# Bias and maximum ahead of copies and z on VectorE, and the last two attention units' turns and values each in one interruption

## The chip, the cores and the metric

The kernel runs on one core of one Trainium2 chip. The metric is the device time of one execution in microseconds (us). Of several runs the median is given. Engines are named as in the profile: PE is TensorE's matmuls, PEld its weight loads, DVE is VectorE, ACT is ScalarE, POOL is GpSimd, SP is the engine that issues most DMAs.

## The reference, cut to what matters

One step of an encoder layer over 320 positions (256 of a prompt, 64 of a running stream), model width 2048, all in float32:

```python
z = rmsnorm(x, ln_g) @ w_in                # 2048 -> 1024 q, 128 k, 128 v, 2 x 1024 gating (u, v)
# group A: 16 heads of 64, 2 key heads; chunks of 64 queries see their own chunk and the 2 before
s = q @ k * HEAD_DIM**-0.5 + bias          # bias: T5 relative positions
m = maximum(max(s), sink)
p = exp(s - m)
w = p / (sum(p) + exp(sink - m))
attn = w @ v
# group B: gelu(zs) -> u, v;  v = rmsnorm(v);  sgu = u * (W_s v + b), chunks of 128 positions
x = x + concat(rmsnorm(attn), rmsnorm(sgu)) @ w_out
x = x + square(relu(rmsnorm(x) @ w_up)) @ w_down
```

Outputs are x for both sets of positions, the new k and v rows, and the normalised v rows of the stream.

## The kernel before, in words

**Weight products.** Activations lie transposed, channels on the 128 partitions and the 320 positions along the free axis. Each matrix is split into a high and a low part. `products` works in pieces: a piece loads 512 rows by 256 columns of a weight (`w_raw`), ScalarE makes the high part (`w_hi`, line 116), VectorE the low part (`w_lo`, line 117), and TensorE runs 24 matmuls of 128x128 by 320 (line 144). There are three buffers each of `w_hi` and `w_lo`. A product of `w_in` has four pieces (96 matmuls) and accumulates in one of two pairs of PSUM banks (`acc`). The products run in the order: q (four, the first with k and v), v of the gating (g = 0 to 3, lines 562 to 571), u of the gating (g = 0 to 3, lines 646 to 665), then w_out, w_up and w_down.

**Interruptions.** `between_pieces` gives functions that run behind a piece: their narrow matmuls stand in TensorE's order between two pieces of weight matmuls. Both `tc.issue_after` and the list `narrow` fix an order of issue on one engine; they add no semaphore wait by themselves. Where nothing fixes it, a planner with a timeline model orders each engine's instructions.

**Attention.** It is done in 8 units: units 0 to 3 for the first key head, 4 to 7 for the second. Units 0 and 4 hold two chunks of queries (two `parts`), the others one. `attend(i)` does three steps of three units in one interruption: the turn of unit i−2 (12 transposes of its probabilities, line 503, into two PSUM banks from the pool `misc`, which has two), the scores of unit i (line 438, into the two score banks), and the values of unit i−3 (line 515, into columns 384 to 511 of the turn's banks, and of the score banks for a second part). Then VectorE adds the bias to the scores (line 460), takes the maximum (line 465) and forms the sink's exponent (`es`, line 466); ScalarE does the exponentials (line 471), POOL multiplies by the reciprocal of the sum (line 481); ScalarE copies values to `ao` (line 523) and VectorE copies the turned probabilities out of the banks to `pts` (line 527), which has two buffers.

`attend(0)` and `attend(1)` stand in the last q product, behind its second and fourth piece; `attend(2 g + 2)` and `attend(2 g + 3)` behind the second and fourth piece of the gating's v product g. So `attend(8)` (turn of unit 6, values of unit 5) stands behind the second piece of v product 3, `attend(9)` (turn of 7, values of 6) behind its fourth, and `attend(10)` (values of 7) behind the second piece of u product 1, together with `prompt_rows`.

**Gating.** `gelu2` reads a product's PSUM pair into z on VectorE (line 549) and alternates between ScalarE (551, 553) and VectorE (552, 554). Squares of v are summed on POOL (`add_square`, line 544), POOL scales v by its gain (line 571). `prompt_rows` turns the v of the two prompt blocks to rows in half-size transposes (`by_halves`, line 582): eight channel groups of block 0 into the misc banks, six of block 1 into the score banks. `by_rows`, one piece later, turns the remaining two of block 1 and the stream's by full transposes (line 599) and copies them out (line 601). `spatial` (lines 611 to 620) applies W_s a piece after that.

Of the kernel before, what the change touches and what calls it, by code (L numbers as in the profile page):

```python
# [11 lines left out]
AF = mybir.ActivationFunctionType  # L12
# [3 lines left out]
P = 128  # L16
# [15 lines left out]
def hymba_step_kernel(ctx: ExitStack, tc: tile.TileContext, i, o):  # L32
# [13 lines left out]
    def misc():  # L46
        return ps_m.tile([P, 512], F32, name="misc", tag="misc")

    def score_bank(p, name="s_ps"):
        return ps_sc.tile([P, 512], F32, name=f"{name}{p}", tag=f"s{p}")  # L50
# [367 lines left out]
    def parts(u):  # L418
        n0 = 0
        for w, (b, kv) in enumerate(groups[u]):  # L420
            yield (w, n0, kv) + blocks[b]
            n0 += len(blocks[b][4])

    probs, ready = {}, []
    room = blk("vnat", [P, 2560])
    vnat = room[:, 0:2048].rearrange("p (t c) -> p t c", t=2)

# [16 lines left out]
    def softmax(u, s_ps):  # L444
        ws = range(len(groups[u]))
        sinks_u = sinks_pj[:, None, :, 2 * groups[u][0][1]:2 * groups[u][0][1] + 2].to_broadcast([P, len(ws), 2, 2])
        if len(ws) == 2:
            nc.vector.tensor_copy(out=s_rows[:, :, :, 64:194:129].rearrange("x p j w -> x w p j"), in_=sinks_u)
        pr = at.tile([P, 2, 3, 2, HD], F32, name="pr", tag="pr", bufs=2)
        nm = at.tile([P, 2, 2, 2], F32, name="nm", tag="nm")  # L450
        den = at.tile([P, 2, 2, 2], F32, name="den", tag="den")
        es = at.tile([P, 2, 2, 2], F32, name="es", tag="es")
        at_col = lambda w: 193 - parts_of_u[w][5]  if w == len(ws) - 1 else 0
        parts_of_u = list(parts(u))
        for w, n0, kv, q0, k0, nk, b0, _ in parts_of_u:
            c = at_col(w)
            for p in range(2):
                for j in range(2):
                    h, at_ = 2 * kv + j, n0 * P + j * nk
                    nc.vector.scalar_tensor_tensor(out=s_rows[:, p, j, c:c + nk], in0=s_ps[p][:, at_:at_ + nk],  # L460
                                                   scalar=rq[:, r_at(h, q0 // HD, p):r_at(h, q0 // HD, p) + 1],
                                                   in1=bias[:, p, h, b0:b0 + nk], op0=ALU.mult, op1=ALU.add)
        for w, n0, kv, q0, k0, nk, b0, _ in parts_of_u:
            c = at_col(w)
            nc.vector.tensor_reduce(out=nm[:, w], in_=s_rows[:, :, :, c:c + nk + 1], axis=AX.X, op=ALU.max, negate=True)  # L465
        nc.vector.tensor_tensor(out=es[:, 0:len(ws)], in0=nm[:, 0:len(ws)], in1=sinks_u, op=ALU.add)
        for w, n0, kv, q0, k0, nk, b0, tiles in parts_of_u:
            c = at_col(w)
            for p in range(2):
                for j in range(2):  # L470
                    nc.scalar.activation(out=pr[:, p, n0:n0 + len(tiles), j],  # L471
                                         in_=s_rows[:, p, j, c:c + nk].rearrange("x (n k) -> x n k", k=HD), func=AF.Exp,
                                         bias=nm[:, w, p, j:j + 1], accum_out=den[:, w, p, j:j + 1])
        nc.scalar.activation(out=es[:, 0:len(ws)], in_=es[:, 0:len(ws)], func=AF.Exp)
        nc.vector.tensor_tensor(out=den[:, 0:len(ws)], in0=den[:, 0:len(ws)], in1=es[:, 0:len(ws)],
                                op=ALU.add)
        nc.vector.reciprocal(out=den[:, 0:len(ws)], in_=den[:, 0:len(ws)])
        for w, n0, kv, q0, k0, nk, b0, tiles in parts_of_u:
            ns = slice(n0, n0 + len(tiles))
            for p in range(2):  # L480
                ready[:] = [nc.gpsimd.tensor_tensor(out=pr[:, p, ns], in0=pr[:, p, ns],
                                                    in1=den[:, w, p, None, :, None].to_broadcast([P, len(tiles), 2, HD]),
                                                    op=ALU.mult).ins]
        probs[u] = pr

    def attend(i, beside=None):

        t, v = i - 2, i - 3
        n = len(groups)
        t, v = t if 0 <= t < n else None, v if 0 <= v < n else None  # L490
        bank = [misc(), misc()] if t is not None else [score_bank(r) for r in range(2)]
        s_ps = [score_bank(p) for p in range(2)] if i < n else None
        hs = [slice(r * HD, (r + 1) * HD) for r in range(2)]

        def behind(mms):
            with tc.issue_after(narrow[-1]):
                narrow.append([mm() for mm in mms][-1].ins)

        if t is not None:
            s = probs.pop(t)  # L500

            def turn(p, n, x):
                return nc.tensor.transpose(out=bank[x][:, (p * 3 + n) * HD:(p * 3 + n + 1) * HD],  # L503
                                           in_=s[hs[x], p, n].rearrange("x j k -> x (j k)"), identity=ident[hs[x], hs[x]])

            behind([lambda p=p, n=n, x=x: turn(p, n, x) for p in range(2) for n in range(3) for x in range(2)])
        if s_ps:
            behind([lambda: scores(i, s_ps)])
        if beside:
            with tc.issue_after(narrow[-1]):  # L510
                outs = beside(bank)
        if v is not None:
            side = {w: [b[:, 384:512] for b in (s_ps if w else bank)] for w in range(len(groups[v]))}
            behind([lambda w=w, n0=n0, n=n, x=x, kv=kv, ts=ts, j=j, p=p:
                    nc.tensor.matmul(out=side[w][j][hs[p]], lhsT=vz[hs[j], x, kv], rhs=pts[v % 2][hs[j], :, p, n0 + n],  # L515
                                     start=n == 0, stop=n == len(ts) - 1)
                    for w, n0, kv, _, _, _, _, ts in parts(v) for n, x in enumerate(ts) for j in range(2) for p in range(2)])
        if s_ps:
            softmax(i, s_ps)
        if v is not None:  # L520
            for w, _, kv, q0, *_ in parts(v):
                for j in range(2):
                    nc.scalar.activation(out=ao[:, 4 * kv + 2 * j:4 * kv + 2 * j + 2, q0:q0 + 64],
                                         in_=side[w][j].rearrange("p (a q) -> p a q", a=2), func=AF.Copy)
        if t is not None:
            for x in range(2):
                nc.vector.tensor_copy(out=pts[t % 2][:, x],
                                      in_=bank[x][:, 0:384].rearrange("k (p n q) -> k p n q", p=2, n=3))

        if beside:  # L530
            for out in outs:
                out()
# [11 lines left out]
            nc.gpsimd.tensor_tensor(out=acc[:, 0:T], in0=acc[:, 0:T], in1=sq, op=ALU.add)  # L544


    def gelu2(ps, out):
        z = sm.tile([P, 2, T], F32, name="z", tag="w2", bufs=4)
        nc.vector.tensor_tensor(out=z, in0=ps[:, :, 0:T], in1=rx[:, None, :].to_broadcast([P, 2, T]), op=ALU.mult)
        c = sm.tile([P, 2, T], F32, name="gc", tag="w2", bufs=4)  # L550
        nc.scalar.activation(out=c, in_=z, func=AF.Square, scale=GELU_R)
        nc.vector.scalar_tensor_tensor(out=c, in0=c, scalar=1.0, in1=z, op0=ALU.add, op1=ALU.mult)
        nc.scalar.activation(out=c, in_=c, func=AF.Tanh, scale=GELU_S)
        nc.vector.scalar_tensor_tensor(out=out, in0=c, scalar=1.0, in1=z, op0=ALU.add, op1=ALU.mult)
# [6 lines left out]
    gvs = room[:, 2048:2560].rearrange("p (a t) -> p a t", a=8)  # L561
    for g in range(4):
        v_ps = product(w_in, 0, KT, 2304 + g * 256, xh, xl, between_pieces={
            1: lambda: (attend(2 * g + 2), norm_q(1, (q2_sq, q3_sq)) if g == 0 else None), 3: lambda: attend(2 * g + 3)})
        gelu2(v_ps, gv[:, 2 * g:2 * g + 2])
        for a in range(2 * g, 2 * g + 2):
            add_square(acc_v, gv[:, a], a == 0)
        for a in ((), (), range(6), range(6, 8))[g]:
            for dst, c in ((gv[:, a, 0:256], slice(0, 256)), (gvs[:, a], slice(256, T))):
                with tc.issue_after(ready[0]):  # L570
                    nc.gpsimd.tensor_scalar(out=dst, in0=gv[:, a, c], scalar1=g_sv[:, a:a + 1], scalar2=None, op0=ALU.mult)
# [50 lines left out]
        narrow.append(mm.ins)  # L622

    def prompt_rows(bank):
        return by_halves(0, 0, 8, [misc() for _ in range(2)]), by_halves(1, 0, 6, bank)

    def rows_norm():
        rv.append(rstd_rows(acc_v, inv_1k, 4 * EPS))
# [1 line left out]
    acc_s = sums("acc_s")  # L630
    parts_a, rm_a = [], rstd_b("rm_a")
    u_pieces = {
        1: {0: rows_norm, 1: lambda: attend(10, prompt_rows), 2: lambda: by_rows((1, 6, 2), (2, 0, 4)),
            3: lambda: spatial(0, 1, 2, 3)},
        2: {1: lambda: spatial(4, 5, 6, 7)},
        3: {1: lambda: rstd(tuple(parts_a), mean_1k, EPS, rm_a)}}
# [160 lines left out]
```

## Time and profile before

| | |
|---|---|
| median of 3 runs | 1237.58 us (1237.36 to 1237.86) |
| the profiled execution's own time | 1238.6 us |
| its span, first to last instruction | 1236.8 us |
| PE busy | 1231.3 us, 8725 matmuls |
| DVE busy | 654.7 us (53%) |
| ACT busy | 492.7 us (40%) |
| POOL busy | 108.0 us (9%) |
| granted TensorE clock | 1.000 |

A row of the timeline has the start in us from the start of the span, the duration, the engine, the line of the kernel, the operation, what it writes and reads, sizes, and how many were merged; in brackets, where there was any, the idle time before it and what ended it. The ends of matmuls are modelled, so differences of their starts are the better measure. The chain follows the execution back from its end to whatever released each step; its rows have the start, the time, and the work. The attention stage lies between 70 and 180 us of the span.

### The profile page before, as it was taken

The numbers are of one execution on the slowest core, as the hardware profiler recorded it, in microseconds if no ns is written. First come the engines' busy times: TensorE is split into PE (matmuls) and PEld (weight loads), VectorE is DVE, ScalarE is ACT, GpSimd is POOL, SyncE is SP. The second block draws the span as 40 slices with busy tenths as digits, with TensorE's granted clock in tenths as the row PEclk, the third lists the DMA queues.
The fourth block names the chain that finished last, engine by engine and source line by source line (L and its number), as shares of the span: only waits on it lengthen the run. The fifth ranks groups of instructions, "written<-read, shape, count | busy, mean of one in ns | idle before, by whom it ended". The sixth has DMA issues, their size and how long they took to land.

```text
span 1236.8 us, 20676 instructions
## 1 busy us (share of the span) xinstructions
PE 1231.3 (100%) x8725; PEld 1222.9 (99%) x8725; DVE 654.7 (53%) x741; ACT 492.7 (40%) x655; POOL 108.0 (9%) x141
## 2 busy tenths in 40 slices
PE   9999999999999999999999999999999999999998
PEld 9999899999999999999999999999999999999998
DVE  7867758877864444444444443444444434444343
ACT  7445556335533432233433332344432333433321
POOL 3144563002200000000000000000000000000000
PEclk9999999999999999999999999999999999999999
DMA  9753346444545444455444444455444454445540
GB/s 284 227 144 102 101 143 208 143 152 146 149 151 153 154 151 145 148 154 153 145 149 151 153 152 143 149 153 153 150 146 150 153 152 144 149 152 164 172 161 32
DMA packets 187917, 188.02 MB, mean 152 GB/s; under 512 B 7600, under 2 KB 187360, under 8 KB 187824
## 3 DMA queue, kind: packets, MB, share of 16 engines
q1 hardware_dynamic: 186528, 185.48, 48.5%
q0 software_dynamic: 864, 0.98, 0.4%
q8 instruction: 68, 1.11, 0.4%
q10 hardware_dynamic: 432, 0.24, 0.1%
q14 instruction: 25, 0.20, 0.0%
HBM read 183.10 MB, written 3.35 MB: 151 GB/s over the span
## 4 chain that ended last, share of the span: by engine, by line
PE 97%; DVE 1%; ACT 1%; issue 0%; DMA 0%; SPq 0%; DVEq 0%; ACTq 0%
PE acc L144 92%; PE q_ps L244 1%; PE acc L244 1%; PE misc L144 1%; PE s_ps L438 0%; DVE w_lo L117 0%; ACT pr L471 0%; ACT w_hi L116 0%; PE misc L503 0%; DMA w_first<-in_w_in 0%; PE misc L515 0%; DVE s_rows L460 0%; DVE nm L465 0%; PE g_ps L611 0%; PE misc L611 0%
## 5 line engine op out<-in xcount | busy, mean ns | idle before, releaser
L117 DVE TENSOR_TENSOR w_lo<-w_raw,w_hi 128x1024 fp32r<-128x1024 f32 x332 | 416.4, 1255 | 438.0 <-ACT w_hi L116 428.2
L116 ACT ACTIVATE w_hi<-w_raw 128x1024 fp32r<-128x1024 f32 x332 | 351.5, 1060 | 675.9 <-PE acc L144 649.7
L144 PE MATMUL acc<-H2H,w_lo 128*128 128x320 f32 x1024 | 316.4, 309 | 0.0
L144 PE MATMUL acc<-H2H,w_hi 128*128 128x320 f32 x1024 | 316.4, 309 | 0.0
L144 PE MATMUL acc<-H2L,w_hi 128*128 128x320 f32 x1024 | 316.4, 309 | 0.0
L144 PE MATMUL acc<-FH,w_hi 128*128 128x320 f32 x992 | 306.5, 309 | 0.0
L144 PE MATMUL acc<-FL,w_hi 128*128 128x320 f32 x992 | 306.5, 309 | 0.0
L144 PE MATMUL acc<-FH,w_lo 128*128 128x320 f32 x992 | 306.5, 309 | 0.0
L144 PEld LDWEIGHTS acc<-H2H,w_lo 128*128 128x128 f32 x1024 | 192.3, 188 | 0.0
L144 PEld LDWEIGHTS acc<-H2H,w_hi 128*128 128x128 f32 x1024 | 192.3, 188 | 0.0
L144 PEld LDWEIGHTS acc<-H2L,w_hi 128*128 128x128 f32 x1024 | 192.3, 188 | 0.0
L144 PEld LDWEIGHTS acc<-FH,w_hi 128*128 128x128 f32 x992 | 186.2, 188 | 0.0
L144 PEld LDWEIGHTS acc<-FL,w_hi 128*128 128x128 f32 x992 | 186.2, 188 | 0.0
L144 PEld LDWEIGHTS acc<-FH,w_lo 128*128 128x128 f32 x992 | 186.2, 188 | 0.0
L144 PE MATMUL acc<-XH,w_hi 128*128 128x320 f32 x352 | 110.3, 313 | 0.0
L144 PE MATMUL acc<-XH,w_lo 128*128 128x320 f32 x352 | 108.9, 309 | 0.1
L144 PE MATMUL acc<-XL,w_hi 128*128 128x320 f32 x352 | 108.7, 309 | 0.0
L144 PEld LDWEIGHTS acc<-XH,w_hi 128*128 128x128 f32 x352 | 66.1, 188 | 2.9 <-issue 2.5
L144 PEld LDWEIGHTS acc<-XH,w_lo 128*128 128x128 f32 x352 | 66.1, 188 | 0.4 <-DVE w_lo L117 0.4
L144 PEld LDWEIGHTS acc<-XL,w_hi 128*128 128x128 f32 x352 | 66.1, 188 | 0.0
L705 DVE SCALAR_TENSOR_TENSOR tf<-acc,r 128x640 f32<-128x640 f32 x32 | 26.4, 825 | 41.8 <-PE acc L144 41.7
L720 DVE TENSOR_TENSOR xT<-xT,acc 128x640 f32<-128x640 f32 x31 | 25.5, 822 | 41.7 <-PE acc L144 41.7
(213 smaller groups left out, 1038.5 us busy)
## 6 DMA issues: line engine op xcount, KB each, us to landing
w_raw<-in_w_up SPq DMA_DIRECT2D x128, 512.0 KB
w_raw<-in_w_down SPq DMA_DIRECT2D x128, 512.0 KB
w_raw<-in_w_in SPq DMA_DIRECT2D x44, 512.0 KB
w_raw<-in_w_out SPq DMA_DIRECT2D x32, 512.0 KB
w_first<-in_w_in SPq DMA_DIRECT2D x14, 256.0 KB
out_yT<-xT SPq DMA_DIRECT2D x7, 320.0 KB
xT<-in_xT SPq DMA_DIRECT2D x8, 160.0 KB
xT<-in_xT SPq DMA_DIRECT2D x4, 320.0 KB
```

The lines of the kernel that those rows point to most:

```text
L116: return (pin(nc.scalar.activation(out=hi, in_=raw, func=AF.Copy)).ins, pin(nc.vector.tensor_tensor(out=lo, in0=raw, in1=hi.bitcast(F32), ...
L117: pin(nc.vector.tensor_tensor(out=lo, in0=raw, in1=hi.bitcast(F32), op=ALU.subtract)).ins)
L144: mm = nc.tensor.matmul(out=out, lhsT=w_[:, k, g * P:(g + 1) * P], rhs=r_(kk), start=(kk == 0 and x == 0), stop=(kk == nk - 1 and x == 2))
L244: mm = nc.tensor.matmul(out=ps[:, 0:T], lhsT=w_[:, j, k, g * P:(g + 1) * P], rhs=r_(a + k), start=(a + k == 0 and x == 0), stop=(a + k == ...
L705: nc.vector.scalar_tensor_tensor(out=t, in0=ps[:, :, 0:T], scalar=0.0, in1=r2[:, None, :].to_broadcast([P, 2, T]), op0=ALU.max, op1=ALU.mult)
L720: nc.vector.tensor_tensor(out=xT[:, a, c], in0=xT[:, a, c], in1=p, op=ALU.add)
```

## The change

- `softmax` keeps the instruction that forms `es` (line 466), the last of a unit's bias and maximum, in a new list `maxed`.
- In `attend`, for turns from unit 1 on that share an interruption with scores, the two copies of the turned probabilities are issued on VectorE after that instruction of the new unit. In `gelu2` of the v products z is issued after it too.
- `attend(8)` takes the turns of units 6 and 7 (the latter into the score banks) and the values of unit 5. It stands behind the third piece of v product 3; nothing stands behind the second and the fourth piece.
- `attend(9)` replaces `attend(10)`, in the same place: the values of units 6 and 7 go to columns 384 to 511 and 256 to 383 of the score banks.
- `prompt_rows` turns four channel groups of block 1 in halves, not six; `by_rows` takes the remaining four in full transposes.

```diff
-    probs, ready = {}, []
+    probs, ready, maxed = {}, [], []
...
-        nc.vector.tensor_tensor(out=es[:, 0:len(ws)], in0=nm[:, 0:len(ws)], in1=sinks_u, op=ALU.add)
+        maxed[:] = [nc.vector.tensor_tensor(out=es[:, 0:len(ws)], in0=nm[:, 0:len(ws)], in1=sinks_u, op=ALU.add).ins]
...
-        t, v = i - 2, i - 3
         n = len(groups)
-        t, v = t if 0 <= t < n else None, v if 0 <= v < n else None
-        bank = [misc(), misc()] if t is not None else [score_bank(r) for r in range(2)]
-        s_ps = [score_bank(p) for p in range(2)] if i < n else None
+        turns = [t for t in ((i - 2,), (n - 2, n - 1), ())[max(0, i - n + 1)] if t >= 0]
+        outputs = [v for v in ((i - 3,), (i - 3,), (n - 2, n - 1))[max(0, i - n + 1)] if v >= 0]
+        pairs = [[misc(), misc()]] if turns else []
+        if i < n or len(turns) > 1 or beside:
+            pairs.append([score_bank(p) for p in range(2)])
+        s_ps = pairs[-1] if i < n else None
+        places = [(pairs[0], 384), (pairs[-1], 384) if len(pairs) > 1 else (pairs[0], 256)]
...
+        for t, bank in zip(turns, pairs):
+            turn(t, bank)
...
-                outs = beside(bank)
+                outs = beside(pairs[0])
+        sides = [(v, [b[:, c:c + P] for b in bank]) + part
+                 for (v, part), (bank, c) in zip(((v, part) for v in outputs for part in parts(v)), places)]
...
+        for t, bank in zip(turns, pairs):
             for x in range(2):
-                nc.vector.tensor_copy(out=pts[t % 2][:, x],
-                                      in_=bank[x][:, 0:384].rearrange("k (p n q) -> k p n q", p=2, n=3))
+                with tc.issue_after(maxed[0]) if t and s_ps else nullcontext():
+                    nc.vector.tensor_copy(out=pts[t % 2][:, x],
+                                          in_=bank[x][:, 0:384].rearrange("k (p n q) -> k p n q", p=2, n=3))
...
-    def gelu2(ps, out):
+    def gelu2(ps, out, behind=None):
         z = sm.tile([P, 2, T], F32, name="z", tag="w2", bufs=4)
-        nc.vector.tensor_tensor(out=z, in0=ps[:, :, 0:T], in1=rx[:, None, :].to_broadcast([P, 2, T]), op=ALU.mult)
+        with tc.issue_after(behind) if behind else nullcontext():
+            nc.vector.tensor_tensor(out=z, in0=ps[:, :, 0:T], in1=rx[:, None, :].to_broadcast([P, 2, T]), op=ALU.mult)
...
-            1: lambda: (attend(2 * g + 2), norm_q(1, (q2_sq, q3_sq)) if g == 0 else None), 3: lambda: attend(2 * g + 3)})
-        gelu2(v_ps, gv[:, 2 * g:2 * g + 2])
+            1: lambda: (attend(2 * g + 2), norm_q(1, (q2_sq, q3_sq)) if g == 0 else None), 3: lambda: attend(2 * g + 3)} if g < 3 else {
+            2: lambda: attend(8)})
+        gelu2(v_ps, gv[:, 2 * g:2 * g + 2], maxed[0])
...
-        return by_halves(0, 0, 8, [misc() for _ in range(2)]), by_halves(1, 0, 6, bank)
+        return by_halves(0, 0, 8, [misc() for _ in range(2)]), by_halves(1, 0, 4, bank)
...
-        1: {0: rows_norm, 1: lambda: attend(10, prompt_rows), 2: lambda: by_rows((1, 6, 2), (2, 0, 4)),
+        1: {0: rows_norm, 1: lambda: attend(9, prompt_rows), 2: lambda: by_rows((1, 4, 4), (2, 0, 4)),
```

More of the change, by code (lines that the diff above doesn't have):

```diff
@@ L497, in behind, with turn @@
                 narrow.append([mm() for mm in mms][-1].ins)
-        if t is not None:
+        def turn(t, bank):
             s = probs.pop(t)
[L502 to L506, printed above, removed]
+            behind([lambda p=p, n=n, x=x: nc.tensor.transpose(
+                        out=bank[x][:, (p * 3 + n) * HD:(p * 3 + n + 1) * HD],
+                        in_=s[hs[x], p, n].rearrange("x j k -> x (j k)"), identity=ident[hs[x], hs[x]])
+                    for p in range(2) for n in range(3) for x in range(2)])
+        for t, bank in zip(turns, pairs):
+            turn(t, bank)
         if s_ps:
@@ L510, in attend @@
             with tc.issue_after(narrow[-1]):
-                outs = beside(bank)
[L512 to L515, printed above, removed]
+                outs = beside(pairs[0])
+        sides = [(v, [b[:, c:c + P] for b in bank]) + part
+                 for (v, part), (bank, c) in zip(((v, part) for v in outputs for part in parts(v)), places)]
+        if sides:
+            behind([lambda v=v, side=side, n0=n0, n=n, x=x, kv=kv, ts=ts, j=j, p=p:
+                    nc.tensor.matmul(out=side[j][hs[p]], lhsT=vz[hs[j], x, kv], rhs=pts[v % 2][hs[j], :, p, n0 + n],
                                      start=n == 0, stop=n == len(ts) - 1)
-                    for w, n0, kv, _, _, _, _, ts in parts(v) for n, x in enumerate(ts) for j in range(2) for p in range(2)])
+                    for v, side, _, n0, kv, _, _, _, _, ts in sides for n, x in enumerate(ts) for j in range(2) for p in range(2)])
         if s_ps:
             softmax(i, s_ps)
[L520 to L525, printed above, removed]
+        for _, side, _, _, kv, q0, *_ in sides:
+            for j in range(2):
+                nc.scalar.activation(out=ao[:, 4 * kv + 2 * j:4 * kv + 2 * j + 2, q0:q0 + 64],
+                                     in_=side[j].rearrange("p (a q) -> p a q", a=2), func=AF.Copy)
+        for t, bank in zip(turns, pairs):
             for x in range(2):
-                nc.vector.tensor_copy(out=pts[t % 2][:, x],
-                                      in_=bank[x][:, 0:384].rearrange("k (p n q) -> k p n q", p=2, n=3))
+                with tc.issue_after(maxed[0]) if t and s_ps else nullcontext():
+                    nc.vector.tensor_copy(out=pts[t % 2][:, x],
+                                          in_=bank[x][:, 0:384].rearrange("k (p n q) -> k p n q", p=2, n=3))
         if beside:
```

## The prediction

> **What bounds the kernel now.** I read the page's chain first, then the chain of waits in order of time, then TensorE's timeline at the places where the chain leaves TensorE, then the other engines there.
>
> ```profile
> PE 97%; DVE 1%; ACT 1%; issue 0%; DMA 0%; SPq 0%; DVEq 0%; ACTq 0%
> ```
>
> TensorE ends nearly everything, so only its own work, the switches between kinds of matmul, and the places where it waits can change the time. In the stage that the change touches the chain leaves it twice:
>
> ```profile
> 118.58 0.81 DVE z L549
> 119.39 1.39 DVE w_lo L117
> ...
> 121.51 1.30 DVE s_rows L460 x4
> ...
> 123.55 0.93 DVE pt L527 x2
> 124.48 0.87 DVE nm L465
> ...
> 127.40 0.96 ACT w_hi L116
> ...
> 129.88 1.84 DVE w_lo L117
> 131.72 1.31 DVE s_rows L460 x4
> ...
> 134.02 0.94 DVE kzv L527 x2
> ...
> 135.00 0.58 PE misc L503 x11
> ```
>
> (Start, us, what.) This is one late story. z of the second gating group goes first on VectorE, unit 5's biased scores come 2.9 us after it, its maximum later still; the exponentials wait for that, the next weights' high parts stand behind the exponentials on ScalarE, their low parts behind those, unit 6's scores behind them, and the copies of a turn, which free the two misc banks, come last. TensorE's next turn then waits for a bank. TensorE's timeline gives the losses (start, duration; starts are what I use):
>
> ```profile
> 114.53 0.31 PE L144 MATMUL acc<-XH,w_lo 128*128 128x320 f32 x1
> ...
> 116.76 0.42 PE L144 MATMUL acc<-XH,w_hi 128*128 128x320 f32 x1
> ...
> 123.75 0.31 PE L144 MATMUL acc<-XH,w_lo 128*128 128x320 f32 x1
> ...
> 126.52 0.41 PE L144 MATMUL acc<-XH,w_hi 128*128 128x320 f32 x1
> ...
> 133.52 0.31 PE L144 MATMUL acc<-XH,w_lo 128*128 128x320 f32 x1
> ...
> 136.98 0.41 PE L144 MATMUL acc<-XH,w_hi 128*128 128x320 f32 x1
> ...
> 143.98 0.31 PE L144 MATMUL acc<-XH,w_lo 128*128 128x320 f32 x1
> 144.22 0.59 PE L503 MATMUL misc<-ident,pr 64*128 64x64 f32 x12
> ...
> 145.55 0.42 PE L144 MATMUL acc<-XH,w_hi 128*128 128x320 f32 x1
> 145.80 0.31 PE L144 MATMUL acc<-XL,w_hi 128*128 128x320 f32 x1
> ...
> 149.32 0.31 PE L144 MATMUL acc<-XL,w_hi 128*128 128x320 f32 x1
> 149.73 0.41 PE L144 MATMUL acc<-XH,w_lo 128*128 128x320 f32 x1
> 149.98 0.31 PE L144 MATMUL acc<-XH,w_hi 128*128 128x320 f32 x1
> ```
>
> From 145.80 to 149.32 there are 24 steps, 0.147 us each: the undisturbed pace. The interruptions of units 5, 6 and 7 hold the same matmuls by the code (a turn of 12 transposes, a full unit's scores, 24 values). They take 2.23 us (114.53 to 116.76), 2.77 and 3.46 from last to first weight matmul. So the second lost 0.54 and the third 1.23 to waiting. At 149.73 one weight matmul came 0.41 after the one before and the next 0.25 after it, against 0.147 each: 0.37 lost to a late low part.
>
> **The change part by part.**
>
> *Turn 7 beside turn 6, one interruption less.* The transposes and value matmuls of units 5, 6 and 7 are the same in number; one entry and one exit go. The entry costs 144.22 − 143.98 − 0.147 = 0.09, the exit 145.80 − 145.55 − 0.147 = 0.10: −0.19 us.
>
> *The two prompt blocks' rows.* The transposes of two channel groups move from the halved form (4 fewer) to the full form (2 more):
>
> ```profile
> 176.54 0.64 PE misc L582 x15
> ...
> 182.09 0.66 PE misc L599 x6
> ```
>
> 4 × 0.64/15 = 0.17 less, 2 × 0.66/6 = 0.22 more: +0.05. ScalarE's copy of these rows grows from 256 to 512 columns:
>
> ```profile
> 183.44 1.03 ACT L601 ACTIVATE vnat<-misc,rs_rows 128x256 f32<-128x256 f32 x2
> 186.10 0.60 PE L611 MATMUL g_ps<-wsT,vnat 128*128 128x128 f32 x4
> ```
>
> The pair (256 and 512 columns) takes 1.03 and ends at 184.47; the first matmul that reads it starts at 186.10. Even another 0.5 stays inside these 1.6 us of weight matmuls; without that cover it would cost at most 0.5. The two further copies of unit 6's values now come in this interruption, not in the one before: ScalarE's number is unchanged. No DMA is added or moved past another, and the program order on SP's and POOL's queues changes only where the planner moves POOL's products, below.
>
> *Bias and maximum ahead of the copies and of z.* No instruction is added; these are orders on VectorE's queue. Behind the maximum now stand the two copies (next TensorE turn waits for them) and z (ScalarE's square waits for it, then the rest of the gelu). For unit 5: after 118.58 there is at worst the low part (1.39) ahead, then scores 1.30 and maximum 0.87, done at 122.1 instead of 125.35, 3.2 us earlier. The copies follow by 123.2 (0.93, with the small sum), ahead of the transposes that want the banks at 123.75 + 0.24 = 123.99. So the 0.54 goes. Next, unit 5's exponentials, the high parts, the low parts and unit 6's scores all move up; copies ended at 134.96 and were wanted at 133.52 + 0.24 = 133.76, so 1.2 of these 3.2 us suffice and the 1.23 goes. What is late next there is nothing that I can name; the margin is about 2.0. z loses the place that it had: it is some 3 us later, and its bank pair is not wanted again before a whole product has run (four pieces of 24 steps, 14.1 us): nothing; each us beyond that would cost one.
>
> For unit 7 the rows are these (VectorE, then POOL):
>
> ```profile
> 138.55 0.81 DVE L549 TENSOR_TENSOR z<-acc,rx 128x640 f32<-128x640 f32 x1
> 139.28 1.21 DVE L117 TENSOR_TENSOR w_lo<-w_raw,w_hi 128x1024 fp32r<-128x1024 f32 x1
> 140.42 0.81 DVE L552 SCALAR_TENSOR_TENSOR gc<-gc,z 128x640 f32<-128x640 f32 x1
> 141.15 1.01 DVE L527 COPY pt<-misc 128x384 f32<-128x384 f32 x2
> 142.08 1.38 DVE L460 SCALAR_TENSOR_TENSOR s_rows<-s_ps,rq,bias 128x192 f32<-128x192 f32 x4
> 143.38 0.81 DVE L554 SCALAR_TENSOR_TENSOR gv<-gc,z 128x640 f32<-128x640 f32 x1
> 144.11 0.95 DVE L465 TENSOR_REDUCE nm<-s_rows 128x4 f32<-128x772 f32 x1
> 144.84 1.82 POOL L544 TENSOR_TENSOR acc_v<-acc_v,sq 128x320 f32<-128x320 f32 x2 [5.53 <-ACT sq L543]
> 147.77 2.59 POOL L481 TENSOR_TENSOR pr<-pr,den 128x384 f32<-128x384 f32 x2 [1.11 <-DVE den L477]
> ```
>
> By starts, z (0.73), gc (0.73), the copies (0.93) and gv (0.73) leave unit 7's path: 3.12 us. The exponentials and then the high parts behind them move with it, so the 0.37 at 149.73 goes.
>
> *The new wait.* Turn 7 now stands three pieces after unit 7's scores, not four. Weight matmuls resume at 136.98; 72 steps with the slow first are 10.7 us, so the merged interruption begins at 147.7, and its transposes of unit 7 (0.09 for the entry, at most 0.59 for turn 6, as at 144.22) at 148.3, on the old clock. Unit 7's probabilities were ready at 147.77 + 2.59 = 150.36; less 3.12 is 147.24. That is 1.1 us in time, with the low part of 139.28 still ahead. So the bounds are 0 (ready) and 2.0 (nothing moved: 150.36 − 148.3). I take 0, since the rows put it on that side, and keep 2.0 for the range.
>
> *The sum.* −0.54 − 1.23 − 0.37 − 0.19 + 0.05 = −2.28 us. The profiled execution was 1238.6 us (span 1236.8, 1.8 around it): 1236.3 by its own clock. The median of the three runs, 1237.58, is 1.0 lower: **1235.3**. All after this stage is weight matmuls that pass the shift on.
>
> *A rule against it.* A row shows what POOL's products do to a low part:
>
> ```profile
> 95.18 2.90 DVE L117 TENSOR_TENSOR w_lo<-w_raw,w_hi 128x1024 fp32r<-128x1024 f32 x1 [0.50 <-ACT w_hi L116]
> 95.38 1.62 POOL L481 TENSOR_TENSOR pr<-pr,den 128x384 f32<-128x384 f32 x2
> ```
>
> 2.90 us beside it, 1.21 at 139.28 without: 1.7 more. The products now come some 3 us sooner and meet other low parts; if one that is wanted at once is met, the sum is −2.28 + 1.7 = −0.6. The Trainium skill, "GPSIMD Engine Reference", Key points, says that POOL shares its SBUF interfaces with VectorE and contends with VectorE instructions that have two SBUF inputs; by that rule the low part (two inputs from SBUF) suffers and the scores and copies (an input from PSUM) do not, and the 2.90 agrees.
>
> **The rivals.**
>
> 1. *A stretched low part holds TensorE.* For it: the row above. Against: with the exponentials some 3 us earlier, the high and low parts behind them come earlier by more than the 1.7. Time 1235.3 + 1.7 = 1237.0.
> 2. *Turn 7 a little late.* If ScalarE puts a pair of high parts (2 × 0.96) ahead of unit 7's exponentials, the margin of 1.1 turns into 0.8 of waiting: 1236.1.
> 3. *The order doesn't do what it says.* It places only the copies and z; nothing keeps the low parts from standing ahead of the scores, as at 129.88. If unit 6's scores stay where they are, the copies, now behind the maximum and its small sum, are no earlier: 0.54 and 1.23 stay, 1237.1. Against: unit 5's 3.2 us come from z, which the order does move.
> 4. *Slower: POOL is the late one.* POOL works in order, and before unit 7's product it did the gating's two sums (144.84). If they keep that place, the product waits for the gelu, which is now behind the maximum: maximum done at 144.11 + 0.95 − 3.12 = 141.9, the copies to 142.9, and from z to the end of the sums before 146.66 − 138.55 = 8.1, at least 6.0 without the copies and a low part between (0.93, 1.14). The sums end at 148.9 to 151.0, the product 2.59 later at 151.5 to 153.6, that is 3.2 to 5.3 after 148.3: 1238.5 to 1240.6. It decides from 2.3 us of lateness on. Against: with the exponentials first, the product has its input several us before the sums have theirs.
>
> **How the numbers follow.** The forecast 0.58 (its own range 1234.9 to 1236.0), rival 1 0.07, rival 2 0.11, rival 3 0.15, rival 4 0.09. About 0.2% (2.5 us) is what a measurement of this kernel can tell from no change: faster is below 1235.1, slower above 1240.1. The likeliest stands 0.2 above the first edge, within the 0.5 us between the three runs shown (1237.36 to 1237.86), so a quarter of its chance falls below: faster 0.15. Of rival 4 the upper third or half is slower: 0.04. The same: 0.81. The range goes from 1234.8 to 1237.8 and leaves out rival 4 and a little of the forecast's edge.
>
> **What would show it.** Right: the interruptions of units 6 and 7 take about 2.25 us from weight matmul to weight matmul; the one with both turns shows 24 transposes and then 24 values without a wait, near 145.9; no low part is waited for in the fourth gating product; VectorE's order after each unit's scores is scores, maximum, small sum, copies, z; POOL's product of unit 7 comes before the sums of the third group. Wrong: TensorE's transposes waiting for pr on POOL (rivals 2 and 4), for the copies (rival 3), or a weight matmul for w_lo (rival 1). The gating's half (misc and score banks full of values and rows) would show as matmuls of line 611 waiting for vnat.

## The result, and the profile after

The changed kernel takes **1235.98 us** (median of 22 runs, 1235.30 to 1237.08); the kernel before, run beside it, took 1237.97 (22 runs). The ratio is 0.9983 [0.9977, 0.9989]: 2.0 us, 0.17%, just inside what was called the same. The forecast was 1235.3. The profiled execution of the changed kernel took 1235.83 us with a span of 1234.0 (before 1238.6 and 1236.8), at the same granted clock of 1.0.

To compare traces I measure the stage from its first score matmul to the first matmul of `spatial` (starts in the chain), so that whatever differs earlier drops out. It went from 186.27 − 70.75 = 115.52 us to 183.45 − 70.49 = 112.96: **−2.56 us**. The other 0.26 of the spans' 2.8 lies ahead of the stage, where the two programs are the same.

The changed kernel's chain (start, us, what) no longer leaves TensorE in this stage. The first line is the page's share by engine:

```profile
PE 99%; DMA 0%; ACT 0%; SPq 0%; DVE 0%; issue 0%; DVEq 0%
```

```profile
135.00 10.76 PE acc L144 x72
...
147.47 21.31 PE acc L144 x144
...
173.87 1.47 PE s_ps L520 x48
```

The 72 and 144 weight matmuls in one piece also show that no low part interrupts them any more. TensorE's timeline at the interruptions of units 6 and 7 (the ones with their scores), the merged one and the one with the gating's halves, and at the full transposes:

```profile
123.49 0.31 PE L144 MATMUL acc<-XH,w_lo 128*128 128x320 f32 x1
...
125.71 0.41 PE L144 MATMUL acc<-XH,w_hi 128*128 128x320 f32 x1
...
132.71 0.31 PE L144 MATMUL acc<-XH,w_lo 128*128 128x320 f32 x1
...
134.93 0.41 PE L144 MATMUL acc<-XH,w_hi 128*128 128x320 f32 x1
...
145.45 0.31 PE L144 MATMUL acc<-XH,w_lo 128*128 128x320 f32 x1
145.69 0.59 PE L504 MATMUL misc<-ident,pr 64*128 64x64 f32 x12
146.11 0.54 PE L504 MATMUL s_ps<-ident,pr 64*128 64x64 f32 x12
146.58 0.89 PE L520 MATMUL misc<-pt,kzv 64*64 64x128 f32 x24
147.40 0.42 PE L144 MATMUL acc<-XH,w_hi 128*128 128x320 f32 x1
...
172.66 0.31 PE L144 MATMUL acc<-XH,w_lo 128*128 128x320 f32 x1
...
175.27 0.42 PE L144 MATMUL acc<-XH,w_hi 128*128 128x320 f32 x1
...
178.74 0.31 PE L144 MATMUL acc<-XH,w_lo 128*128 128x320 f32 x1
...
179.69 0.39 PE L144 MATMUL acc<-XH,w_hi 128*128 128x320 f32 x1
```

The places of before that answer to them are in the prediction's rows, but for the second and the third of the three interruptions that became two, and the full transposes:

```profile
152.91 0.31 PE L144 MATMUL acc<-XH,w_lo 128*128 128x320 f32 x1
...
154.49 0.41 PE L144 MATMUL acc<-XH,w_hi 128*128 128x320 f32 x1
...
176.23 0.31 PE L144 MATMUL acc<-XH,w_lo 128*128 128x320 f32 x1
...
178.31 0.41 PE L144 MATMUL acc<-XH,w_hi 128*128 128x320 f32 x1
...
181.78 0.31 PE L144 MATMUL acc<-XH,w_lo 128*128 128x320 f32 x1
...
182.50 0.39 PE L144 MATMUL acc<-XH,w_hi 128*128 128x320 f32 x1
```

From these rows:

| | before | after | difference |
|---|---|---|---|
| interruption of unit 6 | 2.77 | 2.22 | −0.55 |
| interruption of unit 7 | 3.46 | 2.22 | −1.24 |
| late low part at 149.73 | 0.37 | none | −0.37 |
| three interruptions (143.98 to 145.55, 152.91 to 154.49, 176.23 to 178.31) become two | 5.23 | 4.56 | −0.62 |
| full transposes (before 181.78 to 182.50) | 0.72 | 0.95 | +0.23 |

(In the fourth row one 0.147 that a weight matmul takes anyway comes off each interruption, and one slow step at a resumption, 0.10, goes as well: −0.52 − 0.10.) The five add up to −2.55 of the −2.56.

The order on VectorE and POOL is what the change says (changed kernel's timeline of VectorE at unit 5, then POOL's; at unit 7 scores, maximum, copies and z start at 137.32, 138.74, 139.81 and 140.74):

```profile
118.50 1.38 DVE L460 SCALAR_TENSOR_TENSOR s_rows<-s_ps,rq,bias 128x192 f32<-128x192 f32 x4
119.91 0.96 DVE L465 TENSOR_REDUCE nm<-s_rows 128x4 f32<-128x772 f32 x1
...
120.98 1.01 DVE L532 COPY pt<-misc 128x384 f32<-128x384 f32 x2
121.91 0.81 DVE L555 TENSOR_TENSOR z<-acc,rx 128x640 f32<-128x640 f32 x1
```

```profile
142.41 2.59 POOL L481 TENSOR_TENSOR pr<-pr,den 128x384 f32<-128x384 f32 x2 [6.08 <-PE acc L144]
...
153.32 0.88 POOL L549 TENSOR_TENSOR acc_v<-acc_v,sq 128x320 f32<-128x320 f32 x1
```

Unit 5's copies are done by 121.99; TensorE wants the banks only at 123.73. The product of unit 7 ends at 145.00 and is wanted by the second half of its turn, at 146.30: 1.3 us to spare.

### The profile page after: what moved, and what is told of

Its sections match the earlier page's. It is cut to its first block, busy times and chain, and to the rows that moved or that the text cites. A ratio compares the mean times of both kernels' runs of the same rounds, so it can differ in the third digit from the quotient of the medians.

```text
span 1234.0 us, 20673 instructions
## 1 busy us (share of the span) xinstructions
PE 1229.5 (100%) x8723; PEld 1222.0 (99%) x8723; DVE 656.8 (53%) x741; ACT 492.7 (40%) x655; POOL 109.9 (9%) x141
## 4 chain that ended last, share of the span: by engine, by line
PE 99%; DMA 0%; ACT 0%; SPq 0%; DVE 0%; issue 0%; DVEq 0%
PE acc L144 94%; PE misc L144 1%; PE q_ps L244 1%; PE acc L244 1%; PE s_ps L438 1%; DMA xT<-in_xT 0%; PE misc L504 0%; PE misc L520 0%; PE s_ps L520 0%; PE misc L618 0%; PE g_ps L618 0%; PE misc L334 0%; PE misc L606 0%; SPq L111 0%; PE misc L194 0%; PE misc L193 0%
```

## The experiments

Theory: TensorE waited for one late chain through VectorE; the order (copies and z behind the maximum) takes the waiting away, merging takes an entry, an exit and little more. Rivals: merging alone carries it; one of the two orders alone carries it; the margin of turn 7 isn't what the trace says; POOL's order was the risk. Diffs are against the changed kernel; "stage" is the stretch defined above.

**1. The order without the merging.** All of `attend`, `between_pieces` and `prompt_rows` as before; only `maxed` and its two uses:

```diff
-                nc.vector.tensor_copy(out=pts[t % 2][:, x],
+                with tc.issue_after(maxed[0]) if t and s_ps else nullcontext():
+                    nc.vector.tensor_copy(out=pts[t % 2][:, x],
...
-        gelu2(v_ps, gv[:, 2 * g:2 * g + 2])
+        gelu2(v_ps, gv[:, 2 * g:2 * g + 2], maxed[0])
```

(This diff alone is against the kernel before.)

> The kernel before with the two orders on VectorE alone (copies and z behind the new unit's maximum); interruptions stay as they were (attend(8), (9) and (10)). Theory (late chain on VectorE): the three waits go, 0.54 + 1.23 + 0.37 = 2.1 us faster than before; units 6 and 7 take 2.2 us from weight matmul to weight matmul. Rival (the gain comes from the merged interruptions): at most 0.3 us faster.

Measured: 1236.19 (1235.87 to 1236.7), 0.9981 [0.9972, 0.9990]; stage 184.23 − 70.87 = 113.36, that is −2.16. TensorE waits nowhere in the stage. The interruptions of units 6 and 7 take 2.22 each. The order alone does what was said, and merging on top of it is worth 0.40 in the stage, one trace of each. The medians don't show this 0.40: the order alone lies 2.31 below the kernel before on its chip (1238.50), the changed kernel 1.99 and, in experiment 9, 2.57.

**2. The merging without the order.**

```diff
-                with tc.issue_after(maxed[0]) if t and s_ps else nullcontext():
+                with nullcontext():
...
-        gelu2(v_ps, gv[:, 2 * g:2 * g + 2], maxed[0])
+        gelu2(v_ps, gv[:, 2 * g:2 * g + 2])
```

> The changed kernel without the two orders on VectorE: copies and z go where the planner puts them, interruptions merged. Theory: the waits of units 6 and 7 stay (0.54 and 1.23) and the turn of unit 7 waits for POOL's product, up to 2.0 us; the late low part hides behind that wait; 0.6 us come off for the merging: 0 to 1.3 us slower than before. Rival (the merging alone brings the gain): about 2 us faster than before, no wait for POOL.

Measured: 1240.23 (1238.66 to 1241.74), 1.0015 [1.0006, 1.0024], 1.7 us slower than before; stage +1.46. What TensorE waited for in this kernel's stage (total, times, longest), and where:

```profile
PE s_ps L504 <- POOL pr L481: 1.6, 2, 1.3
PE misc L504 <- DVE kzv L532: 0.8, 1, 0.8
PE misc L504 <- DVE pt L532: 0.2, 1, 0.2
```

```profile
150.15 0.40 PE L504 MATMUL s_ps<-ident,pr 64*128 64x64 f32 x6 [1.30 <-POOL pr L481]
```

This view counts only idle time behind the modelled ends, so the starts are better again. The interruptions of units 6 and 7 take 2.89 and 3.46, so the old waits stay. The merged one takes 4.06 instead of 1.95: turn 7, brought forward by a piece, waits 2.1 us for its product, which is the "nothing moved" end of the prediction's bound (0 to 2.0). So merging alone is a loss; it needs the order.

**3. Only the copies behind the maximum.** z is free:

```diff
-        gelu2(v_ps, gv[:, 2 * g:2 * g + 2], maxed[0])
+        gelu2(v_ps, gv[:, 2 * g:2 * g + 2])
```

> The changed kernel with the copies behind the maximum but z free. Theory (z is what made unit 5 late): z goes ahead of the scores again, the waits of units 6 and 7 stay or grow by 0.2 each since the copies are now last, turn 7 waits about 1.1 us (only the copies, 0.93, have left unit 7's path): 0 to 1 us slower than before. Rival (the copies' place is what counts): as the changed kernel, 2 us faster than before.

Measured: 1236.92 (1235.87 to 1237.48), 0.9986 [0.9977, 0.9995], 1.6 us *faster* than before; stage −1.30. The expectation was wrong. Unit 6's interruption does wait as expected, and no other does:

```profile
PE misc L504 <- DVE pt L532: 0.8, 1, 0.8
```

VectorE at unit 5, and POOL's product of unit 7, in this kernel:

```profile
117.47 0.81 DVE L555 TENSOR_TENSOR z<-acc,rx 128x640 f32<-128x640 f32 x1
...
122.37 0.94 DVE L465 TENSOR_REDUCE nm<-s_rows 128x4 f32<-128x772 f32 x1
...
123.90 1.01 DVE L532 COPY pt<-misc 128x384 f32<-128x384 f32 x2
```

```profile
144.81 2.59 POOL L481 TENSOR_TENSOR pr<-pr,den 128x384 f32<-128x384 f32 x2 [1.09 <-DVE den L477]
```

z still goes ahead, yet unit 5's maximum starts at 122.37, against 124.40 before, which is 1.8 of lead when the 0.28 of this execution's earlier start is taken off. Each unit's copies (0.93) have left the path to its maximum, and the lead accumulates: counted from the stage's start, the last maximum of units 3, 4 and 5 is 0.8, 1.3 and 1.8 earlier than before. The likely reason is that a unit's late scores hold up the exponentials, high parts and low parts that the next unit's scores stand behind. This lead was enough for the interruption of unit 7 (2.23) and for the late low part, but it left unit 5's copies, behind the maximum, at 123.90, later than the banks were wanted (123.71): the interruption of unit 6 takes 3.48 instead of 2.22. Turn 7 is just in time (the product ends at 147.40, its half of the turn starts at 147.54), but only because TensorE comes to it 1.26 later.

**4. Only z behind the maximum.**

```diff
-                with tc.issue_after(maxed[0]) if t and s_ps else nullcontext():
+                with nullcontext():
```

> The changed kernel with z behind the maximum but the copies free. Theory: units 5 and 6 are as early as in the changed kernel, the copies even earlier; unit 7's margin of 1.1 shrinks by at most 0.93 and holds: within 0.3 us of the changed kernel, some 2.3 us faster than before, no wait. Rival (the copies' place counts): the wait of turn 7 for POOL or of units 6 and 7 for banks comes back, at least 0.5 us slower than the changed kernel.

Measured: 1236.58 (1235.9 to 1237.04), 0.9984 [0.9975, 0.9992]; stage −1.88, 0.68 more than the changed kernel's. The expectation was partly missed and its rival came out: the interruptions of units 6 and 7 wait for nothing, but turn 7 does (the merged interruption takes 2.63 instead of 1.95):

```profile
PE s_ps L504 <- POOL pr L481: 0.5, 1, 0.5
```

On VectorE the copies now stand ahead of unit 7's scores (its timeline, and POOL's product):

```profile
138.84 1.01 DVE L532 COPY pt<-misc 128x384 f32<-128x384 f32 x2
139.78 1.38 DVE L460 SCALAR_TENSOR_TENSOR s_rows<-s_ps,rq,bias 128x192 f32<-128x192 f32 x4
```

```profile
144.86 2.59 POOL L481 TENSOR_TENSOR pr<-pr,den 128x384 f32<-128x384 f32 x2 [7.02 <-DVE den L477]
```

Measured in the stage against merging alone (+1.46 over before), the copies' order is worth 2.76, z's 3.34 and both 4.02. They overlap, because any lead beyond what a place needs is spare. Neither is enough by itself: without z's order the interruption of unit 6 waits, without the copies' turn 7 does.

**5. The turns one piece earlier still.** This asks for the size of turn 7's margin:

```diff
-            2: lambda: attend(8)})
+            1: lambda: attend(8)})
```

> The changed kernel with the interruption of both turns behind the second piece of the fourth gating product, not behind the third. Theory: POOL's product of unit 7 ends at 145.0 in any case, the turn wants its second half at 142.8: TensorE waits 2.2 us, the time is 2.2 us above the changed kernel, about that of the kernel before. Rival (the 1.1 us of margin is more than it looks, POOL follows demand): no wait, the same time as the changed kernel.

Measured: 1238.77 (1237.04 to 1240.53), 1.0007 [0.9998, 1.0016]: 2.8 above the changed kernel by medians of two chips, and 1.51 by the profiled stage.

```profile
142.27 0.59 PE L504 MATMUL misc<-ident,pr 64*128 64x64 f32 x12
144.34 0.40 PE L504 MATMUL s_ps<-ident,pr 64*128 64x64 f32 x6 [1.30 <-POOL pr L481]
```

A piece is 3.5 us. In this profiled execution the product came 0.8 earlier than in the changed kernel's (141.69 against 142.41, with a start of the stage 0.1 later), so a margin of 1.3 + 0.8 = 2.1 should leave 1.4 of waiting: measured 1.30 and a stage 1.51 longer. The wait named, its place and its size agree.

**6. POOL's product of unit 7 behind the third group's sums** (rival 4 made true):

```diff
+            if u == 7:
+                later.append(scale)
+            else:
+                scale()
...
+        if g == 2:
+            with tc.issue_after(added):
+                later.pop()()
```

(`scale` is the two multiplications; `added` is the last sum of squares.)

> The changed kernel with POOL's product for unit 7 issued behind the gating's two sums of the third group (the prediction's fourth rival, made true). Theory: the turn of unit 7 waits for POOL; in the changed kernel's trace the squares of that group start at 147.78, so sums 148.2 to 150.0 and the product to 152.6, against 146.35 when the second half of that turn wants it: 6 us slower than the changed kernel, 3.5 us slower than the kernel before. By the prediction's own working 3.2 to 5.3 us slower than the changed kernel. Rival (the wait is not what the margin guards, as the planner would have set the turn later): no more than 1 us.

Measured: 1238.41 (1238.19 to 1239.31), 1.0002 [0.9992, 1.0011]: 2.4 above the changed kernel by medians of two chips, +2.93 in the stage, less than expected. POOL's product ended at 153.52, about where it was expected, but weight matmuls now stand between the two turns (this kernel's TensorE, then its waits). Presumably the planner, whose model also has the product late, put them there:

```profile
146.80 0.41 PE L144 MATMUL acc<-XH,w_hi 128*128 128x320 f32 x1
...
152.40 0.40 PE L509 MATMUL s_ps<-ident,pr 64*128 64x64 f32 x6
```

```profile
PE misc L169 <- POOL acc_v L587: 1.2, 1, 1.2
PE s_ps L509 <- POOL pr L482: 0.4, 1, 0.4
PE acc L144 <- DVE w_lo L117: 0.2, 1, 0.2
```

By starts, the two turns as two interruptions, with the wait between them, cost 1.18 more than the merged one, the sums of the last group, which POOL now does late, 1.33 and a late low part 0.42: together the 2.93. Rival 4's mechanism is real and costs time, but its price with the turns kept together wasn't measured.

**7. The values between the two turns.** TensorE has 0.8 more before it needs unit 7:

```diff
-        for t, bank in zip(turns, pairs):
+        for t, bank in zip(turns[:1], pairs):
             turn(t, bank)
...
+        if turns[1:]:
+            turn(turns[1], pairs[1])
```

> The changed kernel with the order in the merged interruption changed: turn of 6, values of 5, turn of 7 (turns were side by side). No interruption more. Theory (TensorE pays at each change between kinds of narrow matmul, 0.15 us each): the interruption grows by 0.15 to 0.3 us. Rival (only entry and exit against the weight matmuls cost): it keeps its 1.95 us from weight matmul to weight matmul.

Measured: 1236.22 (1235.63 to 1236.42), 0.9982 [0.9973, 0.9991]; the interruption:

```profile
145.98 0.59 PE L504 MATMUL misc<-ident,pr 64*128 64x64 f32 x12
146.49 0.89 PE L520 MATMUL misc<-pt,kzv 64*64 64x128 f32 x24
147.31 0.59 PE L504 MATMUL s_ps<-ident,pr 64*128 64x64 f32 x12
147.83 0.42 PE L144 MATMUL acc<-XH,w_hi 128*128 128x320 f32 x1
```

Its last weight matmul came at 145.74, so it takes 2.09 against 1.95: one more change between kinds of narrow matmul, 0.14. The stage grew by the same 0.14. So there was no wait to gain in the changed kernel, and here the like matmuls were better kept side by side.

**8. One more interruption less.** The scores of units 0 and 1 together, unit 0's in the misc banks:

```diff
+        first = [misc(), misc()] if i == 1 else None
...
+        if first:
+            behind([lambda: scores(0, first)])
...
-                    between_pieces={1: lambda: attend(0), 3: lambda: attend(1)})
+                    between_pieces={1: lambda: attend(1)})
```

> The changed kernel with the scores of units 0 and 1 in one interruption, behind the second piece of the last q product (unit 0 in the misc banks); nothing behind its fourth piece. Theory: one interruption less takes 0.2 (entry and exit) to 0.4 us off, no wait appears since the first turn comes two products' halves later: 0.2 to 0.4 us faster than the changed kernel, about 2.5 us faster than before. Rival (VectorE's longer burst of scores and maxima holds up a low part of the weights): a wait for w_lo on TensorE, 0.3 us or more slower than the changed kernel.

Measured: 1235.58 (1235.05 to 1236.12), 0.9979 [0.9970, 0.9988]; stage −0.36 against the changed kernel.

**9 and 10. Both on one chip.** The changed kernel and the one of experiment 8, both as they are.

> The changed kernel once more, on the chip of the two others of this job. Both theories: 1.5 to 2.5 us faster than before.

> The scores of units 0 and 1 in one interruption, beside the changed kernel on the same chip. Theory (an interruption costs 0.3 to 0.4 us here): 0.3 to 0.5 us below the changed kernel. Rival (the earlier lead was the chip's): no difference.

Measured: 1235.90 (1235.55 to 1236.06), 0.9980 [0.9972, 0.9989], and 1235.62 (1235.33 to 1237.82), 0.9978 [0.9969, 0.9987]. The version with the scores together is 0.28 lower on the same chip, as expected in sign and slightly under the size expected, and has the two lowest medians seen; the two intervals overlap. It has a price: its profiled execution was its slowest run (1237.82), and there the scores waited for the DMA that copies the keys to the other half of the partitions, and a later interruption for copies of VectorE:

```profile
PE misc L438 <- DMA kzv<-kzv: 0.8, 1, 0.8
PE misc L334 <- DVE kzv L537: 0.6, 1, 0.6
```

By starts these two interruptions took 1.45 and 0.65 longer than in experiment 8, and the stage was 1.73 longer than the changed kernel's, not 0.36 shorter.

**11. The order at unit 5 alone.** If all that mattered was the lead which unit 5 gets, the rest follows:

```diff
-                with tc.issue_after(maxed[0]) if t and s_ps else nullcontext():
+                with tc.issue_after(maxed[0]) if i == 5 else nullcontext():
...
-        gelu2(v_ps, gv[:, 2 * g:2 * g + 2], maxed[0])
+        gelu2(v_ps, gv[:, 2 * g:2 * g + 2], maxed[0] if g == 1 else None)
```

> The changed kernel with the two orders only where the prediction's working puts their effect for the first two waits: the copies of the fourth turn behind unit 5's maximum, and z of the second group behind it; everywhere else the planner's order. Theory (unit 5's lead carries on to unit 6, unit 7 needs its own): no wait of units 6 and 7 for banks, but turn 7 waits for POOL as with the merging alone, 2.1 us: about 2.1 us slower than the changed kernel, 0 to 0.5 us faster than before. Rival (the lead is built up over units 3 to 5, as the run with the copies' order alone suggests): a wait of 0.3 us or more at unit 6 or 7 as well, slower than before.

Measured: 1238.62 (1237.03 to 1239.9), 0.9999 [0.9990, 1.0008]; stage +2.08 against the changed kernel. TensorE's waits in the stage:

```profile
PE s_ps L504 <- POOL pr L481: 1.6, 2, 1.3
```

The interruption of unit 6 takes 2.22 and that of unit 7 2.26, 0.04 over its pace: the lead of one unit cures both, as the prediction's chain says. The merged interruption takes 3.99 instead of 1.95, so the theory's 2.1 for turn 7 came out. The lead of unit 5 doesn't cure turn 7; the orders at the other units are needed too, and which of them wasn't tried.

## Why the prediction was right, point by point

- **The late chain.** Right, and its terms are the best hits: 0.54 and 1.23 predicted, 0.55 and 1.24 measured, and experiments 1 and 11 show that the order, and already unit 5's, removes them. The 0.37 of the late low part went too.
- **What gave unit 5 its lead.** Right for z, and incomplete. The prediction put the 3.2 us down to z alone. With z's order alone (experiment 4) unit 5's maximum starts at 121.44 in a stage that starts 0.30 later, 3.3 earlier than the 124.40 of before; experiment 11 gives 3.2. In the changed kernel it starts at 119.91, which is 4.2 when the 0.26 of the earlier start is taken off. Experiment 3 shows what was left out: without z's order, copies that leave each unit's path give 1.8 by unit 5. The working looked at one unit and not at what a unit hands to the next.
- **Turn 7, taken at 0.** Right. The 1.1 was worked out to the first transpose of unit 7, and measured the same way it is 146.11 − 145.00 = 1.1; to the half of the turn that needs the product it is 1.3. Experiments 2 and 5 show the wait that comes without it (2.1 and 1.5 by starts).
- **Merging.** This is the term that was mis-sized: −0.19, and −0.17 for the halved transposes, predicted; −0.62 measured. The 24 transposes side by side took 0.89 (145.69 to 146.58) where two lone sets took 0.52 each, and 48 values of both units 1.47 by the chain where two sets took 0.82 each: 0.15 and 0.17 less. The single starts in the trace of before (143.98 to 145.80) show where this lies, each time over the pace of the neighbours. Entering costs 0.09 at the first transpose and 0.05 more before the third, going over from transposes to values 0.10 and 0.05, leaving 0.11 at the first weight matmul and 0.10 at the second: 0.50 for the interruption that goes. The prediction took the first 0.09 and the last 0.10. So it left out the change from transposes to values (0.15) and the rest of the entry (0.05) and of the exit (0.11). Experiment 7 put one change between narrow kinds back and lost 0.14. The halved transposes gave 0.12, not 0.17 (8 instead of 12 of that last kind); the full ones cost 0.23 for 0.22.
- **The result on the clock.** The sum was −2.28, the stage −2.56, the medians −2.0 beside these 22 runs and −2.57 on the chip of experiment 9 (1238.47, 27 runs, to 1235.90). That the sum lies between the two medians is partly luck, since it has merging 0.26 too small. The profiled execution of before was 0.6 above the median of the 22 runs, and the prediction took its excess off as a constant. It may belong in part to the waits which the change removes, and so make the medians of the 22 runs move less than the traces, but only profiled executions have a trace, so this isn't shown. The level differs too: before's own median was 1237.58 in the first runs and 1237.97 in these, which is 0.4 of the 0.7 by which 1235.98 lies above the forecast.
- **Rivals.** 1: no weight matmul waits for a low part, though low parts do get stretched (a pair of 3.02 at 115.55, with slack behind it). 2: no wait in the changed kernel. 3: refuted, the scores did move. 4: didn't happen, since POOL took unit 7's product 10.9 us ahead of the sums (142.41, 153.32). No matmul of `spatial` waits for `vnat` either.
- **POOL beside VectorE.** The Trainium skill, "GPSIMD Engine Reference", Key points, says that POOL contends with VectorE instructions that have two SBUF inputs. The trace after agrees in kind (a pair of low parts of 4.19 below, against 1.2 each), and scores that read PSUM kept their 1.38 beside POOL's sums (128.64 and 128.23); but it didn't decide the time.

## What to carry to other kernels

When an engine that isn't the bottleneck feeds the one that is, order its queue by who waits: the instruction that starts the longest chain (here the maximum) first, and work with a whole product of slack (z, copies) behind it. Follow the lead through the next rounds before pricing it, since it can grow from one to the next (0.8, 1.3, 1.8 in experiment 3), and price each edit where it is spent: merging was worth 0.40 in the stage with the lead and cost 1.46 without it. When narrow matmuls interrupt a stream of wide ones, count every change of kind, and price it over the steps on both sides of it.

## What the runs showed of the hardware

**Who is held where VectorE and POOL meet changes from run to run.** The same program, the same place, two executions of the changed kernel. First execution, VectorE and POOL:

```profile
94.92 4.19 DVE L117 TENSOR_TENSOR w_lo<-w_raw,w_hi 128x1024 fp32r<-128x1024 f32 x2 [0.50 <-ACT w_hi L116]
```

```profile
95.26 1.62 POOL L481 TENSOR_TENSOR pr<-pr,den 128x384 f32<-128x384 f32 x2
```

Second execution:

```profile
94.92 1.58 DVE L117 TENSOR_TENSOR w_lo<-w_raw,w_hi 128x1024 fp32r<-128x1024 f32 x1 [0.50 <-ACT w_hi L116]
```

```profile
95.28 3.77 POOL L481 TENSOR_TENSOR pr<-pr,den 128x384 f32<-128x384 f32 x2
```

(The first row merges two low parts, of 3.06 and 1.21.) VectorE started 0.3 us before POOL in both. In one the low part is held and the product takes 1.62, in the other the product takes 3.77 and the low part 1.58. In both the stage starts at the same time (70.42); the maximum of unit 2 is at the same time too, that of unit 3, just behind this meeting, 0.7 earlier in the second. Unit 7's product started at 142.41 in the first and at 141.58 in the second. A margin read from one trace has about 0.8 us of play here.

**Waiting kernels scatter.** Kernels whose merged interruption lost 1.5 us or more by starts ranged over 2.9 to 3.5 us (experiments 2, 5 and 11), those without a wait over 0.5 to 1.1 in the same number of runs (experiments 1, 7, 8 and 9; the changed kernel's first 22 runs, twice as many, 1.8). Shorter waits or other ones gave 1.1 to 1.6 (experiments 3, 4 and 6), and experiment 10, with its wait for a DMA in one execution, 2.5. But the kernel before, whose longest wait is 1.24, ranged over 3.25 to 5.91 in 22 to 33 runs, and experiment 3, with one wait of 1.26, over only 1.6, so the length of the wait doesn't order them. That the waits are the cause wasn't tested by itself.

**Small prices,** by the starts of single matmuls (before, 143.98 to 145.80, and experiment 7): from weight matmuls to narrow transposes 0.14 us, between two narrow kinds 0.14 to 0.15, from values back to weight matmuls 0.21.
